# Second half of the output weights split during attention in the feed-forward's ring, and squares of head pairs added on GpSimd

## The chip, the cores and the metric

The kernel runs on one core of a Trainium2 chip, in one launch. A core has TensorE (PE) for matmuls, VectorE (DVE), ScalarE (ACT), GpSimd (POOL), and SyncE (SP), which here only issues transfers. The metric is the device time of the whole program in microseconds, the median of several executions.

## The reference

Two transformer blocks run one after the other on 512 tokens of width 1024, in float32. The change lies in the second:

```python
h = rmsnorm(x, norm_mix_w)
z = h @ w_in                       # u, v, q, keys, values, gates
a = gmlp_group(u, v, ...)          # 512 columns
b = nsa_group(q, k_c, v_c, k_s, v_s, k_w, v_w, g, ...)   # 8 heads of 64 = 512 columns
mix = concatenate([rmsnorm(a, out_norm_a_w), rmsnorm(b, out_norm_b_w)])
x = x + mix @ w_o                  # w_o is 1024 x 1024
h = rmsnorm(x, norm_ffn_w)
x = x + (silu(h @ w_gate) * (h @ w_up)) @ w_down
return rmsnorm(x, final_norm_w)
```

`nsa_group` adds three branches per head with gates: compressed keys, selected blocks, and a window. The rmsnorm of `b` needs the sum of the squares of all 512 columns of a token, so it is known only when the last head is done. The kernel multiplies by `out_norm_b_w` head by head and by the token's factor (`ssq`) after the product with `w_o`.

## The kernel before

**Split operands.** Every float32 matmul is done as three: an operand is split into a rounded part (hi) and the rest (lo), and hi*hi, lo*hi and hi*lo are added in PSUM (L174, L175, L176 in `mm3`). A weight tile arrives by a transfer into `raw` (issued on SP, L140), ACT casts it into `whi` (L116) and DVE, or GpSimd where `eng` says so, subtracts to get `wlo` (L117). `wload` does all of this for one tile of 512 KB. `set_wp` names the pools: a ring of raw tiles and a ring of hi/lo pairs; a transfer waits until its raw tile has been split, a cast until the matmuls that read its pair are done.

**Attention of the second block** (`block2`, `attn_run`). Eight heads, two branches each (`b`: selected, window), are 16 passes; each pass has four blocks of 128 queries, so there are 64 units. A unit is: scores `at` on PE, row maximum on DVE (L702, `amx`), exponential on ACT (L704, `pf`), reciprocal (L713, DVE), normalisation with the gate on GpSimd (L715), transposes `tr` on PE (L721), and the split of the transposed probabilities by ACT (L116, `PT`) and DVE (L117, `PT`). The values' matmuls into `po` follow once a pass. PE writes the scores of a unit up to three units ahead (three `at` banks). Work that is not attention is kept in the list `fill` and is put between units at the numbers that `B2A(left) = 4 + (11 - left) * 5` gives, `left` being the fillers left: queries of the last four heads (2), compressed keys of the second half (1), transposes of the gMLP part `mixA` (4) and its product with the first half of `w_o`, `out_a` (4). Eleven fillers stand at units 4, 9, ..., 54. A scheduler then orders each engine's instructions; the engine executes them in that order.

**After the attention.** `done` closes a head: squares `osq` (ACT), `oB` hi (ACT) and `oB` lo (DVE). Then a matmul with a column of ones sums `osq` over partitions and head pairs (L1843), DVE makes `ssq` (L1844, L240 to L249, L1846), and for each of four token tiles `out_half` makes two PSUM tiles of 12 matmuls (5 `acc` banks) with the second half of `w_o` (`wob`), DVE adds them to `x` (L1865), ACT squares and sums `x` (L1505, `rj`), DVE normalises (`hn`, L1508), PE transposes, ACT and DVE split into `h3T`. The feed-forward's first matmuls need `h3T` of three tiles. Its weights come through the ring `w5r` (3 raw tiles) and the pairs of `w5`; those of the first three feature blocks (6 tiles) are subtracted on GpSimd.

Of the kernel before, what the change touches and what calls it, by code (L numbers as in the profile page):

```python
# [17 lines left out]
OP = mybir.AluOpType  # L18
# [4 lines left out]
NT = S // P  # L23
# [30 lines left out]
class Net:  # L54
# [1526 lines left out]
    def block2(self, x3, out, pre):  # L1581

        nc, a, tc = self.nc, self.a, self.tc
# [5 lines left out]
        w1s, w1 = self.pool("w3", side="right")  # L1589
# [5 lines left out]
        for k0 in (0, 3, 6):  # L1595
            ks = slice(k0, min(k0 + 3, KD))
            n = ks.stop - k0
            raw = self.wraw([(src[:, ks, 1920:2048], slice(0, n), slice(0, P)),
                             (src[:, ks, 2176:2328], slice(0, n), slice(P, 280))], n, 280)
# [38 lines left out]
        for t in range(NT):  # L1638
            with tc.high_priority() if t == 0 else ExitStack():
                norm(t)  # L1640
                h = gp.tile([P, D], F, tag="hn", name=self.name("hn"), bufs=1)
# [87 lines left out]
        for t in range(NT):  # L1729
# [11 lines left out]
        half = lambda r: [[self.wload(wo[(4 * r + k0) * P:(4 * r + k0 + 2) * P, nb * 512:(nb + 1) * 512]  # L1741
                                      .rearrange("(c p) n -> p c n", p=P), 2, 512) for k0 in (0, 2)] for nb in range(2)]
        later = {}

        def queries(f):
            self.set_wp(wqp, 1024, 1, 2)
            self.proj_feat(hT, KD, w_in, [f], ev_q)
            if f == 11:
# [4 lines left out]
                self.set_wp(mx, 1024, 1, 4)  # L1753
                later["wo"] = half(0)

        def out_half(t, r, m, ch, evac):
            ts = slice(t * P, (t + 1) * P)
            for nb in range(2):
                ps = self.acc()
                for k in range(4):  # L1760
                    hi, lo = ch[nb][k // 2]
                    self.mm3(ps, (m[0][:, k, ts], m[1][:, k, ts]), (hi[:, k % 2], lo[:, k % 2]), k == 0, k == 3)
                evac(slice(nb * 512, (nb + 1) * 512), ps)

        def out_a(t):
            out_half(t, 0, later["mixA"], later["wo"],
                     lambda cs, ps: e.tensor_tensor(x3[:, t, cs], x3[:, t, cs], ps, op=OP.add))
# [4 lines left out]
        osq = ap.tile([P, 4, S], F, name="osq")  # L1772
        PT4 = [ap.tile([P, S], F, name=f"PT4{n}") for n in range(2)]

        def compressed(n):
# [24 lines left out]
            for qb in range(NT):  # L1800
# [3 lines left out]
        compressed(0)  # L1804
        each = lambda fn, it: [lambda i=i: fn(i) for i in it]
        fill = (each(queries, (10, 11)) + each(compressed, (1,)) + each(mixa, range(NT))
                + each(out_a, range(NT)))
        heads = []
        pos = {}
        for h in range(8):  # L1810
            n, g = h // 4, h % 4
            rows = slice((h % 2) * 64, (h % 2) * 64 + 64)
            pair = h // 2

            def po_(h=h):
                if h not in pos:
                    pos[h] = self.bank("po")[:64]
                return pos[h]

            def done(po, n=n, g=g, rows=rows, pair=pair):  # L1820
                nc.tensor.matmul(po, vcr[:, g, n], PT4[n], start=False, stop=True)
                nc.scalar.activation(osq[rows, pair], po, AF.Square)
                gcol = obT[rows, pair:pair + 1]
                nc.scalar.activation(oB[0][rows, pair], po, AF.Copy, scale=gcol)
                e.scalar_tensor_tensor(oB[1][rows, pair], po, gcol, oB[0][rows, pair].bitcast(F), op0=OP.mult,
                                       op1=OP.subtract)

            for b in range(2):
                def scores(ps, qs, m, stop, b=b, n=n, h=h):
                    nc.tensor.matmul(ps, QS[h][:, qs], KH[b][n][:, :m], start=True, stop=False)  # L1830
                    nc.tensor.matmul(ps, QS[h][:, qs], KL[b][n][:, :m], start=False, stop=stop)

                heads.append(dict(
                    scores=scores, po=po_, first=b == 0, last=False, done=done if b else lambda po: None,
                    v=lambda kb, b=b, n=n: tuple(VV[i][:, kb, b * P + n * 64:b * P + n * 64 + 64] for i in range(2)),
                    gate=lambda qb, b=b, h=h: gate[:, qb, 8 * (b + 1) + h:8 * (b + 1) + h + 1]))
# [2 lines left out]
        nc.gpsimd.memset(ones, 1.0)  # L1839
        pt = self.trp()  # L1840
        for t in range(NT):
            for c in range(4):
                nc.tensor.matmul(pt[:, t:t + 1], osq[:, c, t * P:(t + 1) * P], ones, start=c == 0, stop=c == 3)  # L1843
        e.tensor_scalar(ssq, pt[:, 0:NT], 1.0 / 512.0, 1e-6, op0=OP.mult, op1=OP.add)  # L1844
        rb = self.rsqrt(ssq, NT)
# [2 lines left out]
        g2s.close()  # L1848
        gms.close()
        cs_.close()  # L1850
        later["s"].close()
        self.set_ps(acc=5, tr=3)
        h3s, hp = self.pool("h3", side="right")
        hT = [hp.tile([P, KD, S], R, name=f"h3T{i}") for i in range(2)]

        w5rs, w5r = self.pool("w5r", side="right")
        w5 = [self.pool(f"w5{i}", side="right") for i in range(self.FP)]
        w1s, w1 = self.pool("w4")
        self.set_wp(w1, 1024, 3, 4)
        wob = half(1)  # L1860
        gs_, gp = self.pool("nrm2")
        gw = self.row(gp, A("norm_ffn_w")[0], D, "gffn")
        for t in range(NT):
            out_half(t, 1, oB, wob,
                     lambda cs, ps: e.scalar_tensor_tensor(x3[:, t, cs], ps, ssq[:, t:t + 1], x3[:, t, cs], op0=OP.mult,  # L1865
                                                           op1=OP.add))
            h = gp.tile([P, D], F, tag="hn", name=self.name("hn"), bufs=2)
            self.rms_tile(x3[:, t], D, gw, h, gp)
            self.to_T(h, hT[0], hT[1], t)
        gs_.close()  # L1870
        w1s.close()
        obs.close()
        w5 += [self.pool(f"w5{i}", side="right") for i in range(self.FP, 5)]
        self.set_wp([p for _, p in w5], 1024, self.FR, 10, rawpool=w5r)

        fs_, fp = self.pool("ff")
        fw = self.row(fp, a["final_norm_w_2"], D, "fnw")
# [28 lines left out]
            w = wd[f0 * P:(f0 + nf) * P]  # L1906
            self.proj_tok(hT2, nf, w, [0, 1], ev, ch=self.resident(nf, w, [0, 1]) if f0 else None)
        fs_.close()
        for st, _ in w5[::-1]:
            st.close()  # L1910
        w5rs.close()
        h3s.close()


@with_exitstack
# [32 lines left out]
```

## Time and profile before

| | |
|---|---|
| median of 3 runs | 2039.54 us (2037.53 to 2048.14) |
| the profiled execution | 2041.58 us |
| its span | 2039.9 us |
| mean granted TensorE clock | 0.950 |
| PE busy | 1851.5 us, 91% of the span |
| DVE busy | 1408.0 us, 69% |
| ACT busy | 1003.7 us, 49% |
| GpSimd busy | 557.8 us, 27% |

The span is the time from the first to the last instruction in the profile; the device time of that execution is 1.7 us longer. Times in rows are microseconds from the span's start. The second block's attention ends at about 1617 us, and its feed-forward runs from 1663 us to the end. PEclk 1.00 is TensorE's full 2.4 GHz, 0.50 is 1.2 GHz.

### The profile page before, as it was taken

Reading aid. Unit: us, or ns where it says so; the run is one execution under the profiler, and the core shown is the slowest. Engines: PE = TensorE matmul, PEld = TensorE weight load, DVE = VectorE, ACT = ScalarE, POOL = GpSimd, SP = SyncE. Lnnn points to the kernel's source line nnn. Section 1 sums busy time; section 2 is a strip of 40 time slices with the busy share of each in tenths; the row PEclk is TensorE's granted clock in tenths of the full one; section 3 lists DMA queues with packets and bytes.
Section 4 is the critical chain, followed back from the end, with each engine's and each line's share of the span. In section 5 each row is a group of like instructions: output and inputs, shape, how many; then the busy total and the mean of one; then the engine's idle time right before and its main releaser. Section 6 shows DMA issues by size and latency. Waiting matters only on the chain.

```text
span 2039.9 us, 25354 instructions
## 1 busy us (share of the span) xinstructions
PE 1851.5 (91%) x8971; PEld 1425.2 (70%) x8971; DVE 1408.0 (69%) x2610; ACT 1003.7 (49%) x1456; POOL 557.8 (27%) x459
## 2 busy tenths in 40 slices
PE   7699898998989998998989999759999799999998
PEld 6577676786766666666666666558777578888886
DVE  7966776777789888987888888574566563332333
ACT  3363555336337666765767766335355432222320
POOL 6633111200544433433443434230032300000000
PEclk8899999999989999998999999879989899999999
DMA  5223324633459999999999999724210243233311
GB/s 146 64 81 104 114 63 145 216 109 105 188 208 337 334 337 331 350 335 320 344 334 345 341 344 337 200 69 127 75 42 1 83 126 102 93 93 99 98 52 42
DMA packets 175580, 368.92 MB, mean 181 GB/s; under 512 B 17548, under 2 KB 113112, under 8 KB 150872
## 3 DMA queue, kind: packets, MB, share of 16 engines
q1 hardware_dynamic: 154240, 309.19, 44.5%
q0 software_dynamic: 17920, 52.98, 10.6%
q10 hardware_dynamic: 3288, 5.07, 0.8%
q8 instruction: 73, 1.20, 0.2%
q14 instruction: 59, 0.48, 0.1%
HBM read 337.83 MB, written 37.75 MB: 184 GB/s over the span
## 4 chain that ended last, share of the span: by engine, by line
PE 57%; DVE 16%; DMA 13%; ACT 7%; issue 5%; POOL 1%; another core or an unknown queue 1%; DVEq 0%; ACTq 0%; SPq 0%; POOLq 0%
PE acc L174 16%; PE acc L175 15%; PE acc L176 15%; DMA raw<-in_w_exp_gu_dram 5%; DVE wlo L117 3%; ACT whi L116 2%; DMA accd<-y,idx 2%; DMA gx<-x2d,idx 2%; PE tr L721 1%; PE tr L1263 1%; ACT xt L116 1%; DVE xt L117 1%; PE po L175 1%; PE po L176 1%; PE po L174 1%
## 5 line engine op out<-in xcount | busy, mean ns | idle before, releaser
L116 ACT CAST whi<-raw 128x1024 fp32r<-128x1024 f32 (+3 forms) x292 | 411.2, 1413 | 392.1 <-PE acc L175 196.1
L117 DVE TENSOR_TENSOR wlo<-raw,whi 128x1024 fp32r<-128x1024 f32 (+3 forms) x281 | 478.7, 1707 | 166.8 <-ACT whi L116 159.2
L1311 POOL DMA_INDIRECT accd<-y,idx x63 | 128.8, 2045 | 375.7 <-DMA accd<-y,idx 139.2
L174 PE MATMUL acc<-whi,gT 128*96 128x512 f32 x512 | 212.3, 415 | 0.0
L176 PE MATMUL acc<-whi,gT 128*96 128x512 f32 x512 | 207.6, 405 | 0.0
L175 PE MATMUL acc<-wlo,gT 128*96 128x512 f32 x512 | 206.8, 404 | 0.0
L1254 POOL DMA_INDIRECT gx<-x2d,idx x64 | 163.4, 2553 | 54.9 <-issue 16.7
L117 DVE TENSOR_TENSOR xt<-raw,xt 128x2048 fp32r<-128x2048 f32 x64 | 146.5, 2289 | 13.6 <-ACT xt L116 9.0
L174 PE MATMUL acc<-xt,aT 128*96 128x512 f32 x256 | 110.2, 430 | 42.0 <-ACT aT L116 41.8
L174 PE MATMUL acc<-h3T,whi 128*128 128x512 f32 (+2 forms) x368 | 140.5, 382 | 0.2 <-ACT h3T L116 0.2
L175 PE MATMUL acc<-h3T,whi 128*128 128x512 f32 (+2 forms) x368 | 140.5, 382 | 0.1
L176 PE MATMUL acc<-h3T,wlo 128*128 128x512 f32 (+2 forms) x368 | 140.5, 382 | 0.0
L116 ACT CAST xt<-raw 128x2048 fp32r<-128x2048 f32 x64 | 122.1, 1908 | 0.4
L176 PEld LDWEIGHTS acc<-whi,gT 128*96 128x96 f32 x512 | 85.5, 167 | 36.8 <-issue 1.1
L175 PEld LDWEIGHTS acc<-wlo,gT 128*96 128x96 f32 x512 | 86.2, 168 | 33.0 <-issue 0.2
L174 PEld LDWEIGHTS acc<-whi,gT 128*96 128x96 f32 x512 | 86.7, 169 | 32.3 <-issue 0.9
L1306 ACT ACTIVATE y<-acc,wsl 96x512 f32<-96x512 f32 x63 | 43.3, 687 | 126.2 <-PE acc L176 122.5
L175 PE MATMUL acc<-xt,aT 128*96 128x512 f32 x256 | 105.1, 411 | 0.0
L117 DVE TENSOR_TENSOR gT<-tr,gT 128x384 fp32r<-128x384 f32 x128 | 68.9, 549 | 40.6 <-ACT gT L116 40.4
L176 PE MATMUL acc<-xt,aT 128*96 128x512 f32 x256 | 90.7, 395 | 0.0
L174 PEld LDWEIGHTS acc<-xt,aT 128*96 128x96 f32 x256 | 42.8, 167 | 66.2 <-ACT aT L116 52.4
L116 ACT CAST gT<-tr 128x384 fp32r<-128x384 f32 x128 | 58.2, 480 | 55.5 <-PE tr L1263 55.5
(673 smaller groups left out, 4475.2 us busy)
## 6 DMA issues: line engine op xcount, KB each, us to landing
raw<-in_w_exp_gu_dram SPq DMA_DIRECT2D x128, 1024.0 KB, 9.6
raw<-in_w_exp_down_dram SPq DMA_DIRECT2D x64, 1024.0 KB, 10.6
raw<-in_w_in_dram SPq DMA_DIRECT2D x40, 512.0 KB, 4.1
raw<-in_w_gate_dram SPq DMA_DIRECT2D x22, 512.0 KB, 3.9
raw<-in_w_up_dram SPq DMA_DIRECT2D x22, 512.0 KB, 4.0
raw<-in_w_down_dram SPq DMA_DIRECT2D x22, 512.0 KB, 3.8
gsp<-sg POOLq DMA_DIRECT2D x16, 256.0 KB, 2.4
raw<-in_w_s_glu_dram SPq DMA_DIRECT2D x16, 256.0 KB, 4.2
```

What stands on the lines that cost most here:

```text
L116: first = nc.scalar.copy(hi, src)
L117: return first, (eng or nc.vector).tensor_tensor(lo, src, hi.bitcast(F), op=OP.subtract)
L174: mm(out, l[0], r[0], start=start, stop=False)
L175: mm(out, l[0], r[1], start=False, stop=False)
L176: mm(out, l[1], r[0], start=False, stop=stop)
L721: nc.tensor.transpose(pt[:, kb], pf[:, kb * P:(kb + 1) * P], self.ident)
L1254: nc.gpsimd.indirect_dma_start(out=gx, out_offset=None, in_=x2d, in_offset=bass.IndirectOffsetOnAxis(ap=idx, axis=0), bounds_check=S - 1, ...
L1263: nc.tensor.transpose(pt[:, c], gx[:, (c0 + c) * P:(c0 + c + 1) * P], self.ident[:C, :C])
L1306: nc.scalar.activation(y[:, :512], ps, AF.Copy, scale=w)
L1311: nc.gpsimd.indirect_dma_start(out=acc, out_offset=bass.IndirectOffsetOnAxis(ap=idx, axis=0), in_=y, in_offset=None, compute_op=OP.add)
```

## The change

`second` becomes a twelfth filler, the last one. It closes `mixA` (whose last reader is `out_a`), opens the feed-forward's raw ring and its first four hi/lo pairs in the freed space, and loads and splits the four tiles of the second half of `w_o` there; the feed-forward continues in the same ring with ten pairs. Since `B2A` counts fillers left, twelve fillers stand at units -1 (taken at the first), 4, ..., 54, so all eleven old ones move forward by five units and `second` takes unit 54. `squares`, called after head 5, adds `osq` of head pairs 0, 1 and 2 with two GpSimd additions of 128x512, so the ones-matmuls read 2 tiles instead of 4.

```diff
+        def second():
+
+            later["s"].close()
+            later["raw"] = self.pool("w5r", side="right")
+            later["w5"] = [self.pool(f"w5{i}", side="right") for i in range(self.FP)]
+            self.set_wp([p for _, p in later["w5"]], 1024, self.FR, 4, rawpool=later["raw"][1])
+            later["wob"] = half(1)
+
+        def squares():
+            nc.gpsimd.tensor_tensor(osq[:, 0], osq[:, 0], osq[:, 1], op=OP.add)
+            nc.gpsimd.tensor_tensor(osq[:, 0], osq[:, 0], osq[:, 2], op=OP.add)
...
-                + each(out_a, range(NT)))
+                + each(out_a, range(NT)) + [second])
...
+                if h == 5:
+                    squares()
...
-            for c in range(4):
+            for c in (0, 3):
...
-        later["s"].close()
...
-        w5rs, w5r = self.pool("w5r", side="right")
-        w5 = [self.pool(f"w5{i}", side="right") for i in range(self.FP)]
-        w1s, w1 = self.pool("w4")
-        self.set_wp(w1, 1024, 3, 4)
-        wob = half(1)
+        w5rs, w5r = later["raw"]
+        w5 = later["w5"] + [self.pool(f"w5{i}", side="right") for i in range(self.FP, 5)]
+        self.set_wp([p for _, p in w5], 1024, self.FR, 10, rawpool=w5r)
+        self.wslot = 2 * self.FP - 1
+        wob = later["wob"]
```

**ACT near the end of the attention.** These are rows of the changed kernel: `at_15304` and `at_15321` are the last two units of head 6's first pass, `at_15355` to `at_15437` its second pass, `at_15466` on head 7; `raw_15413`, `15419`, `15425`, `15431` are the four tiles of `w_o`.

```order
L704 ACTIVATE pf_15327,amx_15325<-at_15321,amx_15325 128x512
L116 CAST whi_15415<-raw_15413 128x1024
L704 ACTIVATE pf_15361,amx_15359<-at_15355,amx_15359 128x128
L116 CAST whi_15421<-raw_15419 128x1024
L1834 ACTIVATE osq<-po_15232 64x512
L1836 ACTIVATE oB_12871<-po_15232,obT 64x512
L116 CAST PT_15329<-tr_15365 128x256
L704 ACTIVATE pf_15376,amx_15374<-at_15370,amx_15374 128x256
L116 CAST PT_15329<-tr_15380 128x384
L116 CAST whi_15427<-raw_15425 128x1024
L116 CAST PT_15329<-tr_15396 128x512
L704 ACTIVATE pf_15392,amx_15390<-at_15386,amx_15390 128x384
```

No `whi` stood there before; the four casts of this half of `w_o` stood behind the last `oB` of the attention. The fourth (`whi_15433`) comes right after these rows, ahead of the exponential of `at_15437`.

**DVE at the same place, changed kernel.** These are the subtractions of the same four tiles among the units' maxima (L702) and splits (`PT`).

```order
L117 TENSOR_TENSOR wlo_15416<-raw_15413,whi_15415 128x1024
L713 RECIPROCAL amx_15359<-amx_15359 128x1
L117 TENSOR_TENSOR wlo_15422<-raw_15419,whi_15421 128x1024
L1837 SCALAR_TENSOR_TENSOR oB_12872<-po_15232,obT,oB_12871 64x512
L117 TENSOR_TENSOR PT_15330<-tr_15365,PT_15329 128x256
L117 TENSOR_TENSOR PT_15330<-tr_15380,PT_15329 128x384
L702 TENSOR_REDUCE amx_15390<-at_15386 128x1
L117 TENSOR_TENSOR wlo_15428<-raw_15425,whi_15427 128x1024
L117 TENSOR_TENSOR PT_15330<-tr_15396,PT_15329 128x512
L117 TENSOR_TENSOR wlo_15434<-raw_15431,whi_15433 128x1024
L702 TENSOR_REDUCE amx_15441<-at_15437 128x1
```

Before, these four subtractions stood behind `ssq` (L1846), three ahead of the first addition to `x` (L1865) and one ahead of the second.

**DVE between the second and the third token tile's `hn`, changed kernel.** `wlo_16219`, `16250`, `16286` and `16317` are weights of the feed-forward (tiles 7 to 10 of its order); `hn_15806` is tile 1.

```order
L1508 SCALAR_TENSOR_TENSOR hn_15806<-x_12783,rs_15811,gffn 128x1024
L1878 SCALAR_TENSOR_TENSOR x_12784<-acc_15852,ssq,x_12784 128x512
L117 TENSOR_TENSOR wlo_16219<-raw_16216,whi_16218 128x1024
L117 TENSOR_TENSOR h3T_15703<-tr_15824,h3T_15702 128x4x128
L117 TENSOR_TENSOR h3T_15703<-tr_15831,h3T_15702 128x4x128
...
L117 TENSOR_TENSOR wlo_16250<-raw_16247,whi_16249 128x1024
...
L117 TENSOR_TENSOR wlo_16286<-raw_16283,whi_16285 128x1024
...
L117 TENSOR_TENSOR wlo_16317<-raw_16314,whi_16316 128x1024
```

Tile 2's `hn` stands ten rows behind the last of these. Before, no weight stood between the `hn` of tile 1 and that of tile 2; two of the feed-forward's stood ahead of the `hn` of tile 0.

## Rows read from the trace of the kernel before

**Rows 1.** Windows: length, PE, PEld, DVE, ACT, POOL busy (instructions), clock, DMA.

```profile
1591.50:1596.60 5.10, 5.10 (x38) 3.81 (x37) 3.58 (x9) 2.86 (x10) 0.77 (x1) 1.00 0.78 210
1596.60:1617.40 20.80, 16.84 (x80) 10.78 (x79) 7.99 (x24) 8.57 (x24) 4.83 (x8) 0.84 0.31 101
...
1620.00:1625.00 5.00, 2.20 (x8) 1.60 (x8) 3.49 (x4) 3.89 (x5) 3.45 (x2) 0.50 0.00 1
1625.00:1630.00 5.00, 0.00 (x0) 0.00 (x0) 4.83 (x6) 1.05 (x1) 4.48 (x3) 0.50 0.36 104
1630.00:1635.00 5.00, 1.25 (x3) 1.05 (x4) 4.79 (x10) 0.00 (x0) 1.36 (x1) 0.50 0.13 6
1635.00:1640.00 5.00, 5.00 (x13) 3.86 (x13) 2.12 (x3) 1.26 (x2) 0.00 (x0) 0.52 0.99 283
1645.00:1650.00 5.00, 5.00 (x23) 4.03 (x22) 4.67 (x13) 3.32 (x6) 0.75 (x1) 1.00 0.82 233
```

**Rows 2.** PE in time order: start, duration, operation, count, idle before and its releaser.

```profile
1591.23 0.40 PE L176 MATMUL acc<-whi,mixA 128*128 128x512 f32 x1
1591.47 0.39 PE L1830 MATMUL at<-KH,QS 128*128 128x512 f32 x1
1596.61 0.31 PE L1830 MATMUL at<-KH,QS 128*128 128x128 f32 x1
1604.13 0.76 PE L721 MATMUL tr<-ident,pf 128*128 128x128 f32 x5 [1.20 <-DVE PT L117]
1605.43 0.48 PE L174 MATMUL po<-PT,VV 128*64 128x512 f32 x1 [0.54 <-ACT PT L116]
1606.16 0.69 PE L175 MATMUL po<-PT,VV 128*64 128x512 f32 x1 [0.25 <-DVE PT L117]
1617.43 3.98 PE L1843 MATMUL tr<-ones,osq 128*128 128x1 f32 x26 [0.68 <-ACT osq L1822]
1633.76 0.79 PE L175 MATMUL acc<-wlo,oB 128*128 128x512 f32 x1 [10.91 <-DVE wlo L117]
1663.22 0.62 PE L174 MATMUL acc<-h3T,whi 128*128 128x384 f32 x2 [0.24 <-ACT h3T L116]
1668.15 1.06 PE L292 MATMUL tr<-ident,hn 128*128 128x128 f32 x8
```

**Rows 3.** DVE in time order, from the squares' sum to the third tile's norm.

```profile
1621.64 2.28 DVE L240 TENSOR_SCALAR rs<-ssq 128x4 f32<-128x4 f32 x1
1632.40 0.17 DVE L1846 COPY ssq<-rs 128x4 f32<-128x4 f32 x1
1632.48 3.50 DVE L117 TENSOR_TENSOR wlo<-raw,whi 128x1024 fp32r<-128x1024 f32 x3
1660.49 1.28 DVE L1508 SCALAR_TENSOR_TENSOR hn<-x,rs,gffn 128x1024 f32<-128x1024 f32 x1
```

**Rows 4.** POOL in time order: the feed-forward's first six weights.

```profile
1621.55 6.95 POOL L117 TENSOR_TENSOR wlo<-raw,whi 128x1024 fp32r<-128x1024 f32 x3 [14.18 <-ACT whi L116]
1640.98 4.77 POOL L117 TENSOR_TENSOR wlo<-raw,whi 128x1024 fp32r<-128x1024 f32 x2 [9.62 <-ACT whi L116]
```

**Rows 5.** Groups by shape (busy us, mean ns): tail's ACT, then DVE and ACT after it.

```profile
L116 ACT CAST PT<-tr 128x512 fp32r<-128x512 f32 x4 | 2.3, 586 | 2.1 <-PE tr L721 2.1
L704 ACT ACTIVATE pf<-at,amx 128x512 f32<-128x512 f32 x3 | 2.1, 694 | 0.6 <-DVE amx L702 0.4 <-DVE amx L713 0.2
...
L117 DVE TENSOR_TENSOR wlo<-raw,whi 128x1024 fp32r<-128x1024 f32 x7 | 8.4, 1221 | 0.3 <-ACT whi L116 0.2
L1865 DVE SCALAR_TENSOR_TENSOR x<-acc,ssq,x 128x512 f32<-128x512 f32 x8 | 6.0, 747 | 6.5 <-PE acc L176 6.4
L117 DVE TENSOR_TENSOR h3T<-tr,h3T 128x512 fp32r<-128x512 f32 x8 | 5.2, 687 | 2.3 <-ACT h3T L116 2.2
L116 ACT CAST whi<-raw 128x1024 fp32r<-128x1024 f32 x7 | 7.3, 1052 | 12.1 <-DMA raw<-in_w_o_dram 9.0 <-DMA raw<-in_w_up_dram 2.3 <-DMA raw<-in_w_gate_dram 0.8
```

**Rows 6.** The page's DMA issues: count, KB each, median us from issue to landing.

```profile
raw<-in_w_gate_dram SPq DMA_DIRECT2D x22, 512.0 KB, 3.9
```

More of the change, by code (lines that the diff above doesn't have):

```diff
@@ L1818, in po_, with done @@
                 return pos[h]
-            def done(po, n=n, g=g, rows=rows, pair=pair):
+            def done(po, n=n, g=g, rows=rows, pair=pair, h=h):
                 nc.tensor.matmul(po, vcr[:, g, n], PT4[n], start=False, stop=True)
@@ L1870, in block2 @@
         gs_.close()
-        w1s.close()
         obs.close()
-        w5 += [self.pool(f"w5{i}", side="right") for i in range(self.FP, 5)]
-        self.set_wp([p for _, p in w5], 1024, self.FR, 10, rawpool=w5r)
         fs_, fp = self.pool("ff")
@@ L1908, in block2 @@
         fs_.close()
-        for st, _ in w5[::-1]:
+        for st in [st for st, _ in w5[:self.FP - 1:-1]] + [h3s] + [st for st, _ in w5[self.FP - 1::-1]] + [w5rs]:
             st.close()
-        w5rs.close()
-        h3s.close()
 @with_exitstack
```

## The prediction

> **What bounds the kernel now.** The page first: PE is busy for 91% of the span, so what can be won is where PE waits or runs at the low clock. The windows show one such place, the seam between the second block's attention and its feed-forward [rows 1]: from 1620 to 1635 PE works 3.45 of 15 us, from 1635 to 1640 it is full but at a clock of 0.52 (13 matmuls where 1645 to 1650 has 23). Before it, in the attention's tail, PE works 16.84 of 20.8 us at 0.84; once the feed-forward runs, nothing is left to win. PE in time order says what ends each wait [rows 2]: the tail's gaps end on DVE and ACT splits of probabilities (1.20, 0.54, 0.25), the last ones-matmuls start at 1617.43 and their 26 records take 3.98 us, and the product with the second half of w_o waits 10.91 us for the first `wlo`. That wait is the one the change aims at. DVE in time order shows what stands before that `wlo` [rows 3]: a chain of operations on 128x4 numbers for `ssq`, one of them 2.28 us, ready at 1632.57, and only then three `wlo`. GpSimd runs the feed-forward's `wlo` meanwhile [rows 4]. So the wait has two causes in series, `ssq` and the splits; taking the splits away leaves `ssq`, and everything that leads to the feed-forward's first matmul (additions to x, norms, transposes) needs `ssq` too.
>
> **The change, part by part.** I count on the axis of the profiled execution: 2041.58 us, of which the span is 2039.9; it lies 2.0 us above the median, to which the sum is carried over at the end. All casts of a weight are 1.05 us on ACT and all its subtractions 1.22 us on DVE [rows 5].
>
> **1. The seam after the attention.** Let the last ones-matmuls start at the same 1617.43. The 26 records become 14 (half of the 16 matmuls), 2.1 us at the same 0.153 each: 1.8 us earlier. PE then goes straight into the product: its weights are there. But DVE's `ssq` chain stands beside GpSimd's first `wlo` as before: these began at 1621.55, right behind the ones-matmuls [rows 4], and the chain was done 11.0 us later. Now they begin at about 1619.2, behind the first cast, and run as before; so `ssq` at 1630.2 instead of 1632.57.
> From there to tile 2's `hn` I add DVE's queue as its order stands: six additions 0.75, two finished tiles' `h3T` 4 x 0.69, three `hn` 1.28, four weights of the feed-forward 1.22 (they now stand there, before they didn't), the last tile's two additions, some 35 small operations at 0.17: 4.5 + 2.8 + 3.8 + 4.9 + 1.5 + 6.0 = 23.5, and two waits of about 1.2 for ACT's `rj`, since tile 1's second addition now stands behind tile 0's `hn`. That is 1656 to 1657, against 1661.8 [rows 3]. PE has 60 product matmuls done by the first `hn` (five banks) and waits for DVE from there; DVE has the pace, and the four splits taken away were replaced by four others. The first feed-forward matmul follows 1.45 us behind, as before (1663.22): 1658.3. Tile 3's `hn` is next in DVE's queue, so its transposes are done by 1659.8, where before their 1.0 us stood inside the feed-forward, at 1668.15. So the feed-forward flows from 1659.8 instead of 1664.2: **-4.4**.
> Two things take from that. PE waits some 7 us for tile 2 (1649.5 to 1656.8). After the wait of 10.91 the clock was at 0.50 and the next 5 us had 13 matmuls instead of 23 [rows 1]; at the feed-forward's start the same costs 2.2 to 2.9 us: **+2.5** (0 to 2.9). And GpSimd's fifth and sixth `wlo`, 4.77 us, which ran beside DVE's second product waits before [rows 4], now fall on tile 0's norm, because ACT casts them only behind the first `rj`: **+1** (0 to 4.8).
> The 128x4 operations that took 2.28 beside GpSimd's `wlo` and 0.17 without it [rows 3, 4] agree with the Trainium skill, "SBUF — State Buffer", section "SBUF: two separate sides": DVE and GpSimd share a port pair as an exclusive lock, and the loser is blocked for the whole instruction. By that rule alone the last term would be the full +4.8; the additions from PSUM at 1640 to 1645 of 0.75 show no such delay.
>
> **2. The tail of the attention.** The transfers of w_o go into the space of `mixA`, whose last reader is the end of `out_a`; there is no reading them earlier. With the fillers five units forward, `out_a` ends 43 PE instructions earlier, about 4.5 us of matmuls (rows of 512 columns stand 0.24 apart, the rest in proportion): at 1587.0 instead of 1591.5. Call this T. A tile of 512 KB takes 3.9 us to land [rows 6]: T+4.3. ACT reaches the first cast at T+3.4 and waits 0.9. From there its queue has, in order, cast, exponential, cast, squares, copy, two splits with an exponential between, cast, split, exponential, cast: with 0.6 to 0.9 for an exponential and 0.3 to 0.6 for a split [rows 5], the exponential of the unit before head 7 ends at T+9.4 and the fourth cast at T+13.4. DVE's fourth `wlo` ends at T+14.6, the maximum queued behind it at 15.3, its exponential at 16.2. PE's scores run three units ahead and each needs the exponential of three units before: it waits for the first of these 2.9 us, for splits 0.9 and 0.7, for the last exponential 1.7. I get PE to head 7's second pass at T+17.9. Before, that score stood at 1596.61 [rows 2]; the same PE work from T is 4.5 + 5.1 = 9.6 with no wait (PE 5.10 of 5.10 [rows 1]). Loss 8.3; but the tail after it had waits of 1.20 + 0.54 + 0.25 on the same engines, which a PE that comes later doesn't meet again: **+6.3**. Lower bound: in those 5.1 us ACT was free for 2.2 and DVE for 1.5 [rows 1], the passes around have as much, and if the units in flight absorb the rest, +1. Upper bound: no wait is saved and the landing is late, +10.
> The low clock began in the tail at about 1605, after these gaps [rows 1, 2]; with larger gaps earlier, it begins earlier, beside waits that hide part of it: **+1** (0 to 8).
>
> **3. The rest.** `squares` are two GpSimd operations of half a weight's size, 2.32 / 2 = 1.2 us each by [rows 4], one of them in the stretch just counted, where GpSimd is nearly idle (0.77 of 5.1): 0, at most +1 through what it holds up. The fillers' forward move at the attention's start, where PE is full, and the second compressed part, whose DVE chain has less PE work before its transposes: **+0.5** (0 to 2.5). The feed-forward's ring with six pairs ahead: nothing, PE is full there before.
>
> Sum: -4.4 + 2.5 + 1 + 6.3 + 1 + 0.5 = +6.9; since I may count waits twice where ACT and DVE are late together, I take **+6**: 2047.6 for the profiled execution, **2045.5** by the median.
>
> **The rivals.** *PE has the pace at the seam (faster).* If DVE's weights and small operations slip between PE's, the seam is 96 product matmuls at 0.234 (22.5 us), 2.8 for those at the low clock, four tiles of transposes (4.2), 2.1 and 1.5 at the ends: 1617.43 + 33.1 = 1650.5 against 1664.2, -13.7, with the tail at its lower bound +1 and 0.5 for the rest: 2027.3. For it: the wait of 10.91 is the largest of this stretch. Against: DVE was busy 4.67 of 5 us from 1645 [rows 1] and gets no less work. It decides from -12 at the seam. Chance 0.13.
> *The low clock spreads through the tail (slower).* If the first wait of 2.9 us at T+6.5 brings the clock down and the tail never gets it back, the matmuls of the tail that ran at full speed before (some 7.5 us up to 1605, and 3.7 of the stretch before) take twice as long where no wait hides it: up to +11 in place of +1, which with waits beside it I put at +8: 2052.5. From 4.5 us of such loss on it is slower by over 0.5%. For it: 1605 to 1617 ran low although PE was busy most of the time. Chance 0.22.
> *The splits vanish in the tail, and the seam is DVE's (no change).* Tail +1, seam -1 to -4: 2036 to 2040. It is part of the forecast's case: together 0.65.
>
> **How the numbers follow.** 0.5% is 10.2 us, about what a measurement of this kernel can tell from no change. Faster by more 0.13, within 0.65, slower by more 0.22. The terms' lower bounds (seam -4.4 or a little below with the lock not met, tail +1) give 2036, their upper bounds 2058; the faster rival lies at 2027. 8 in 10 lie between 2030 and 2055.
>
> **What the profile of the changed kernel would show.** The wait of 10.91 is gone and the product starts behind the ones-matmuls; if it stays, part 1 is wrong from its start. DVE is busy without a break from `ssq` to tile 2's `hn`, and PE waits there for `hn`; if PE is full, the first rival is right. In the tail, the four `whi` end between T+5 and T+14 and PE waits 5 to 9 us more than before between `out_a` and the last ones-matmuls, which start near 1624; if they start by 1619, part 2 is wrong. The clock at the feed-forward's first 5 us: half by my count. A tail at 0.5 from some 1594 on is the second rival.

## The result and the profile after

The change is slower. In six runs of each the changed kernel took 2059.12 us (median, 2051.81 to 2060.5), the kernel before 2040.24 (2037.53 to 2048.14); the ratio on record is 1.0066, 95% interval 1.0045 to 1.0087, that is +13.5 us (+9 to +18). The profiled execution took 2055.44 us, 13.9 more than that of before. The two medians lie 18.9 us apart, 0.93%, just outside that interval, so the size is less certain than the direction; what follows goes by the ratio and the profiles. The forecast was +6, within 0.5%; slower by more than 0.5%, where the ratio lies, had a chance of 0.22.

For every kernel of this study the second block can be cut at four instructions: the first mask matmul of the compressed keys, the last matmul of `out_a`, the last group of ones-matmuls, and the first feed-forward matmul. The lengths between them, each the difference of two starts in PE's time order, in us:

| kernel | to out_a's end | out_a's end to ones | attention, sum | ones to feed-forward | feed-forward to end |
|---|---|---|---|---|---|
| before | 124.8 | 26.2 | 151.0 | 45.8 | 376.7 |
| changed | 124.8 | 38.2 | 163.0 | 45.8 | 377.5 |

The attention is 12.0 us longer, the seam (ones to feed-forward) no shorter, the feed-forward 0.9 longer; the other 0.9 of the 13.9 lies ahead of the second block's attention, where nothing was changed.

The attention can be cut further, at the mask matmul of the second half's compressed keys and at the first score of head 7's second pass. PE in these four stretches, before (length, busy, instructions, clock, DMA share and GB/s):

```profile
1466.39:1499.66 33.27, 33.25 (x183) 0.90 0.16 48
1499.66:1591.23 91.57, 87.60 (x504) 0.94 0.06 18
1591.23:1596.61 5.38, 5.38 (x39) 1.00 0.74 200
1596.61:1617.43 20.82, 16.83 (x81) 0.84 0.31 100
```

And in the changed kernel:

```profile
1467.28:1495.20 27.92, 26.44 (x139) 0.88 0.21 57
1495.20:1592.12 96.92, 91.72 (x507) 0.91 0.05 17
1592.12:1608.95 16.83, 13.33 (x79) 1.00 0.70 218
1608.95:1630.32 21.37, 17.09 (x80) 0.84 0.01 2
```

About as many instructions stand between the second compressed keys and `out_a`'s end in both (504 and 507), and they take 5.3 us longer: PE is busy for 4.1 us more, at a lower mean clock, and idle for 1.2 more. The instructions that the forward move took away ahead of the keys make that stretch 5.4 us shorter; where they stand now, between `out_a`'s end and head 7's second pass, they make it 11.5 us longer. The rest of the tail is 0.6 us longer.

PE of the changed kernel in time order, with idle time ahead and its releaser:

```profile
1507.96 1.12 PE L1813 MATMUL tr<-ident,p 128*128 128x128 f32 x4 [2.38 <-DVE p L1809]
...
1592.12 0.40 PE L176 MATMUL acc<-whi,mixA 128*128 128x512 f32 x1
...
1601.12 0.33 PE L1844 MATMUL at<-KH,QS 128*128 128x128 f32 x1 [1.31 <-ACT pf L704]
1602.92 0.44 PE L174 MATMUL po<-PT,VV 128*64 128x512 f32 x1 [0.45 <-ACT PT L116]
...
1607.17 0.44 PE L1844 MATMUL at<-KH,QS 128*128 128x384 f32 x1 [1.14 <-ACT pf L704]
...
1617.04 0.77 PE L721 MATMUL tr<-ident,pf 128*128 128x128 f32 x5 [1.20 <-DVE PT L117]
...
1630.32 1.72 PE L1857 MATMUL tr<-ones,osq 128*128 128x1 f32 x14 [0.68 <-ACT osq L1834]
...
1653.91 1.97 PE L292 MATMUL tr<-ident,hn 128*128 128x128 f32 x8 [7.85 <-DVE hn L1508]
...
1674.40 1.94 PE L292 MATMUL tr<-ident,hn 128*128 128x128 f32 x8 [5.87 <-DVE rs L249]
1676.16 0.69 PE L174 MATMUL acc<-h3T,whi 128*128 128x384 f32 x1
1676.69 1.94 PE L292 MATMUL tr<-ident,hn 128*128 128x128 f32 x8
```

The wait of 10.91 us for the first `wlo` [rows 2] is gone, and the product starts behind the ones-matmuls. In its place PE waits 7.85 us for tile 0's norm and 5.87 for tile 2's (the row names `rs`, which DVE worked on next; tile 2's `hn` ends at 1674.26). DVE of the changed kernel in time order shows what those norms waited for:

```profile
1632.28 2.31 DVE L240 TENSOR_SCALAR rs<-ssq 128x4 f32<-128x4 f32 x1
...
1636.97 2.32 DVE L247 TENSOR_TENSOR rs<-rs 128x4 f32<-128x4 f32 x1
...
1639.72 2.34 DVE L247 TENSOR_TENSOR rs<-rs 128x4 f32<-128x4 f32 x1
...
1643.09 0.17 DVE L1860 COPY ssq<-rs 128x4 f32<-128x4 f32 x1
...
1647.16 2.18 DVE L245 SCALAR_TENSOR_TENSOR rs<-rs,rs 128x1 f32<-128x1 f32 x1
1649.37 2.26 DVE L249 SCALAR_TENSOR_TENSOR rs<-rs,rs 128x1 f32<-128x1 f32 x1
1651.67 0.22 DVE L245 SCALAR_TENSOR_TENSOR rs<-rs,rs 128x1 f32<-128x1 f32 x1
...
1664.58 1.23 DVE L117 TENSOR_TENSOR wlo<-raw,whi 128x1024 fp32r<-128x1024 f32 x1 [1.73 <-ACT whi L116]
...
1670.95 1.22 DVE L117 TENSOR_TENSOR wlo<-raw,whi 128x1024 fp32r<-128x1024 f32 x1
...
1672.98 1.28 DVE L1508 SCALAR_TENSOR_TENSOR hn<-x,rs,gffn 128x1024 f32<-128x1024 f32 x1
```

GpSimd's instructions beside them, in the same view of the same kernel:

```profile
1632.18 7.09 POOL L117 TENSOR_TENSOR wlo<-raw,whi 128x1024 fp32r<-128x1024 f32 x3 [11.90 <-PE tr L1857]
1639.64 2.40 POOL L117 TENSOR_TENSOR wlo<-raw,whi 128x1024 fp32r<-128x1024 f32 x1 [0.37 <-ACT whi L116]
1646.98 4.64 POOL L117 TENSOR_TENSOR wlo<-raw,whi 128x1024 fp32r<-128x1024 f32 x2 [4.93 <-DVE rs L241]
```

`ssq` is ready 12.9 us after the ones-matmuls began (before: 15.1 [rows 2, 3]). GpSimd's fifth and sixth subtraction now stand right on the chain of tile 0's norm: the same operation takes 2.18 us beside them and 0.22 behind them. Last, windows of 5 us of the changed kernel at the attention's start, with the sum over 1465 to 1530, and at the feed-forward's (columns as in [rows 1]):

```profile
1495.00:1500.00 5.00, 4.42 (x38) 4.30 (x37) 2.92 (x11) 2.33 (x9) 2.93 (x5) 0.91 0.30 105
1500.00:1505.00 5.00, 4.46 (x16) 3.26 (x17) 3.38 (x5) 1.65 (x4) 0.00 (x0) 0.50 0.00 0
1505.00:1510.00 5.00, 2.62 (x12) 2.05 (x11) 3.90 (x10) 1.93 (x4) 0.70 (x1) 0.50 0.30 105
1510.00:1515.00 5.00, 4.68 (x15) 2.98 (x15) 1.44 (x5) 2.72 (x7) 1.20 (x2) 0.50 0.34 105
...
sum 65.00, PE 58.71 PEld 43.98 DVE 37.97 ACT 32.62 POOL 11.88; mean PE 4.52 PEld 3.38 DVE 2.92 ACT 2.51 POOL 0.91
...
1675.00:1680.00 5.00, 5.00 (x21) 4.57 (x20) 4.06 (x7) 2.35 (x4) 0.00 (x0) 0.50 0.31 83
```

And the kernel before at the attention's start, in the same windows:

```profile
1500.00:1505.00 5.00, 5.00 (x39) 4.70 (x37) 2.74 (x9) 3.15 (x8) 2.00 (x4) 0.83 0.38 105
1505.00:1510.00 5.00, 5.00 (x21) 3.89 (x21) 3.85 (x8) 1.41 (x3) 0.00 (x0) 0.50 0.34 101
1510.00:1515.00 5.00, 2.57 (x13) 1.68 (x13) 4.30 (x11) 2.74 (x7) 1.73 (x2) 0.84 0.06 7
...
sum 65.00, PE 61.90 PEld 48.36 DVE 42.10 ACT 37.58 POOL 18.89; mean PE 4.76 PEld 3.72 DVE 3.24 ACT 2.89 POOL 1.45
```

The compressed keys of the second half, 32 columns to a matmul, stand at 1495 to 1501 in the changed kernel and at 1500 to 1504 in that before. Behind them the clock is at 0.50 for three windows in the one, for one window in the other, and PE is idle 6.3 of the 65 us instead of 3.1. The feed-forward of the changed kernel, too, begins at 0.50, behind PE's wait for tile 2.

### The profile page after: what moved, and what is told of

It is laid out like the page before. It is cut to its first block, busy times and chain, and to the rows that moved or that the text cites. A ratio compares the mean times of both kernels' runs of the same rounds, so it can differ in the third digit from the quotient of the medians.

```text
span 2053.7 us, 25334 instructions
## 1 busy us (share of the span) xinstructions
PE 1858.2 (90%) x8955; PEld 1426.8 (69%) x8955; DVE 1412.1 (69%) x2610; ACT 1003.4 (49%) x1456; POOL 560.0 (27%) x461
## 4 chain that ended last, share of the span: by engine, by line
PE 59%; DVE 15%; DMA 11%; ACT 8%; issue 5%; POOL 2%; another core or an unknown queue 1%; ACTq 0%; DVEq 0%; SPq 0%; POOLq 0%
PE acc L174 17%; PE acc L175 16%; PE acc L176 16%; DMA raw<-in_w_exp_gu_dram 6%; ACT whi L116 3%; DVE wlo L117 2%; DMA gx<-x2d,idx 2%; PE tr L1263 1%; PE tr L721 1%; DVE xt L117 1%; ACT xt L116 1%; DMA accd<-y,idx 1%; PE po L175 1%; PE tr L292 1%; DVE rs L245 1%
## 5 line engine op out<-in xcount | busy, mean ns | idle before, releaser
L117 DVE TENSOR_TENSOR gT<-tr,gT 128x384 fp32r<-128x384 f32 x128 | 68.8, 548 | 36.7 <-ACT gT L116 36.7
```

The costliest lines, as they stand in the source:

```text
L117: return first, (eng or nc.vector).tensor_tensor(lo, src, hi.bitcast(F), op=OP.subtract)
```

## The experiments

The theory that the trace after suggests: three places lose, each by its own cause. The forward move of the fillers costs at the attention's start, the splits of w_o cost in the tail, and at the seam GpSimd's subtractions and four weights of the feed-forward eat what the earlier splits gain. Rivals: one of the two, forward move or splits, is the whole loss; or the short DVE operations are long for another reason.

One profile does not tell small differences in the attention from chance. Three kernels without early splits and with the fillers in their old units have 151.0 us (before), 149.4 (`e4_squares`) and 150.1 (`e8_sq_dve`); three with early splits and the old units have 150.5 (`e2_keep`), 152.7 (`e7_keep_dve`) and 152.4 (`e11_six`).

**Fillers forward alone** (`e1_shift`), on the kernel before:

```diff
-                + each(out_a, range(NT)))
+                + each(out_a, range(NT)) + [lambda: None])
```

> The kernel before with a twelfth filler that does nothing, so that the eleven others stand five units earlier as in the change; the loads and splits of w_o and the squares stay where they were. Theory (three places: start of the attention +5, tail +8 by the splits of w_o, seam +1): the start's loss alone shows, out_a ends about 5 us later than its five units' move would give, the tail is 5 units longer without fillers and loses 0 to 2 more, so 2045 to 2048, 0.25% to 0.4% over before. Rival (the tail's loss comes from its having no filler for ten units, not from the splits): all of the start's and tail's loss is here, 2052 to 2054. Rival (the forward move costs nothing, the splits do all): 2040.

Measured 1.0039 (1.0024 to 1.0054), +8 us; the attention is 156.8 us, +5.8. So the forward move alone costs about half of the 12.0 us lost in the attention, with no split of w_o in it: the second rival is out, and the first, which expected all of the loss here, is not met either. PE in the four stretches of this kernel:

```profile
1466.81:1493.49 26.68, 25.03 (x139) 0.94 0.21 60
1493.49:1588.96 95.47, 89.72 (x506) 0.93 0.06 18
1588.96:1603.97 15.01, 13.25 (x82) 1.00 0.69 210
1603.97:1623.62 19.65, 15.53 (x81) 0.91 0.00 1
```

The stretch behind the compressed keys is 3.9 us longer than before. The displaced instructions add 9.6 us to the tail (15.01 instead of 5.38) and take 6.6 off the stretch ahead of the keys.

**Splits without the move** (`e2_keep`), on the changed kernel:

```diff
-                + each(out_a, range(NT)) + [second])
+                + each(out_a, range(NT - 1)) + [lambda: (out_a(NT - 1), second())])
```

> The changed kernel with the eleven old fillers at their old units and the loads and splits of w_o called in unit 54, right behind the last out_a. Theory: the start's 5 us are back, the tail still has ACT's and DVE's splits and waits for its transfers: 2045 to 2049, 0.25% to 0.45% over before. Rival (forward move is the whole loss): 2038 to 2041. Rival (the splits are the whole loss): 2052 to 2054 as the changed kernel.

Measured 1.0009 (0.9997 to 1.0021). The attention is 150.5 us, not longer than before: out_a's end to the ones-matmuls grew by 1.3, and the stretch before it was shorter by 1.8. The expected 2045 to 2049 was too much. By the six attentions named above the splits alone cost 1.7 us on average, about what single profiles differ by; the rival, that the forward move is the whole loss, is nearer for the attention. The seam is 45.9, as in the changed kernel.

**Squares alone** (`e4_squares`), the two GpSimd additions and the shorter ones-matmuls on the kernel before:

> The kernel before with the squares alone. Theory: the ones-matmuls take 2 us less, GpSimd's first weight and the ssq chain begin 2 us earlier, the wait for the first wlo ends earlier by the same: 2037 to 2039. Rival (the chain is set by GpSimd's casts, not by the ones-matmuls, or the two additions hold up the attention): 2040 to 2042.

Measured 0.9982 (0.9971 to 0.9993), -3.7 us. The profile has 2.9 us of it at the seam (42.9 instead of 45.8): `ssq` follows 12.7 us behind the start of the ones-matmuls instead of 15.1.

**No subtraction on GpSimd** (`e6_dve`), on the changed kernel:

```diff
-                    hi, lo = self.wload(..., KD, P, eng=nc.gpsimd if f0 + fi < 3 else None)
+                    hi, lo = self.wload(..., KD, P, eng=None)
```

> The changed kernel with the feed-forward's first six subtractions on DVE and none on GpSimd. Theory (DVE's short operations wait out GpSimd's subtractions): ssq is ready 5 us after the ones-matmuls begin instead of 12.9, the first tile's norm loses its two operations of 2.2 us, but DVE gets six times 1.22: tile 2's norm ends some 38 us after the ones-matmuls instead of 43.9, so 5 to 6 us less than the changed kernel. Rival (the long operations are slow for another reason, such as a wait inside DVE): ssq stays at 12 to 13 and the six subtractions come on top, 5 to 7 us more than the changed kernel.

Measured 1.0009 (0.9995 to 1.0023): 11.7 us less than the change by the two ratios (1.0066 - 1.0009 = 0.0057 of 2044), more than the 5 to 6 expected. The profiles explain 9.3: ones to feed-forward 37.3 instead of 45.8, and 376.8 instead of 377.5 behind it. DVE in time order:

```profile
1633.97 0.17 DVE L1860 COPY ssq<-rs 128x4 f32<-128x4 f32 x1
...
1647.80 1.28 DVE L1508 SCALAR_TENSOR_TENSOR hn<-x,rs,gffn 128x1024 f32<-128x1024 f32 x1
1653.09 1.28 DVE L1508 SCALAR_TENSOR_TENSOR hn<-x,rs,gffn 128x1024 f32<-128x1024 f32 x1
1663.12 1.28 DVE L1508 SCALAR_TENSOR_TENSOR hn<-x,rs,gffn 128x1024 f32<-128x1024 f32 x1
```

The ones-matmuls began at 1629.00, so `ssq` took 5.1 us instead of 12.9. With six more subtractions of 1.22 us in its own queue, DVE still has tile 2's norm 8.5 us earlier behind the ones-matmuls (34.1 instead of 42.7). The rival (slow for another reason) is out. The remaining 2.4 us of the 11.7 are within the two intervals.

**Both repairs** (`e7_keep_dve`): the old fillers' units and no subtraction on GpSimd, on the changed kernel.

> The changed kernel with the old fillers at their old units (as the second run) and the feed-forward's first six subtractions on DVE (as the fourth). Theory: the two repairs are in different places and add up, the attention ends as in the second run, some 2 us behind the kernel before, and the seam is 8 to 9 us shorter than the change's: 9 to 11 us less than before, ratio 0.9945 to 0.9955. Rival (DVE, which now has all subtractions, takes back at the seam what the old fillers give): 0.998 to 1.001.

Measured 0.9972 (0.9956 to 0.9989), -5.7 us, between the two expectations. Ones to feed-forward is 39.3, and tile 2's norm comes 10.4 us after tile 1's: four weights of the feed-forward stand between them.

**The same on the kernel before with squares** (`e8_sq_dve`): w_o stays behind the attention.

> The kernel before with the squares and with the feed-forward's first six subtractions on DVE; the loads of w_o stay behind the attention. Theory: ssq is ready 5 us after the ones-matmuls begin instead of 12.6, but in DVE's order three of the six stand ahead of the first wlo of w_o, and three behind it: of the 7.6 us some 4 are given back before the product starts and 3 behind, so 0 to 2 us less than the squares alone, ratio 0.997 to 0.9985. Rival (without GpSimd's subtractions the seam shortens by the whole 7.6 here too): 0.994.

Measured 0.9962 (0.9943 to 0.9982), -7.8 us, more than the theory gave; ones to feed-forward 38.7, 4.2 less than with the squares alone. So with GpSimd out of the way, and four weights of the feed-forward still between the norms in `e7_keep_dve`, the early splits of w_o bring nothing at the seam that late ones don't (38.7 here, 39.3 there).

**The first three fillers forward** (`e9_start`) and **the last eight forward** (`e10_tail`), on the kernel before:

```diff
-    B2A = staticmethod(lambda left: 4 + (11 - left) * 5)
+    B2A = staticmethod(lambda left: 4 + (11 - left) * 5 - 5 * (left > 8))     # e9_start
+    B2A = staticmethod(lambda left: 4 + (11 - left) * 5 - 5 * (left <= 8))    # e10_tail
```

> The kernel before with only the first three fillers (the last queries and the second half's compressed keys) five units earlier; the other eight stay. Theory: the start's part of the forward move, two waits and a longer stretch at the low clock around the compressed keys, 2 to 5 us: ratio 1.001 to 1.0025; the tail is as before. Rival (the forward move costs only because the tail has no filler): 1.000.

> The kernel before with only the last eight fillers (the transposes and out_a) five units earlier; the first three stay. Theory: the tail is 5 units longer without fillers, from out_a's end to the ones-matmuls 34 to 35 us instead of 26.2 plus the 4.5 that moved there, so 3 to 4.5 us: ratio 1.0015 to 1.0025. Rival (the start alone): 1.000.

Measured 1.0025 (1.0003 to 1.0047) and 0.9992 (0.9977 to 1.0008). In the profiles the first comes to `out_a`'s end 4.6 us later than before and gets 2.9 back in the tail: +1.7 for the attention. The second comes there 9.0 us earlier and has a tail of 36.3 us: +1.1. The two parts sum to 2.8, the whole move costs 5.8, and with the splits 8.8 to 12.0 (163.0, 162.8 and 159.8 us in the changed kernel, `e6_dve` and `e12_six_after`). In the profiles the parts don't add up to the whole; by the times, +5.1 us (+1 to +10) and -1.6 (-5 to +2) against +8 (+5 to +11), they may. By the timed runs the start is the part that costs; the expected loss of the tail alone was not found.

**Weights 7 to 10 behind the norms** (`e12_six_after` on the changed kernel; `e11_six` the same on `e7_keep_dve`): the feed-forward's first half uses six pairs of the ring and leaves w_o's four alone.

```diff
                 for w in (wg, wu):
+                    if not f0 and self.wslot == 2 * len(w5) - 1:
+                        self.wslot = 2 * self.FP - 1
```

> The changed kernel with that one edit: weights 7 to 10 of the feed-forward are split behind the norms; fillers, squares and GpSimd's subtractions as in the change. Theory: tile 2's norm starts 35 to 37 us after the ones-matmuls instead of 42.7; 6 to 8 us less than the changed kernel, ratio 1.0025 to 1.004. Rival (GpSimd's six subtractions alone set the seam): 1.006 as the change.

> The kernel of the seventh run (old fillers in place, no subtraction on GpSimd) whose feed-forward leaves the four pairs of w_o alone until its second half, so that its weights 7 to 10 are split only when the first pairs come free, behind all four norms. Theory (four subtractions of 1.22 us and the waits for their casts stand between tile 1's and tile 2's norm and delay the feed-forward): tile 2's norm starts some 6 us earlier, 30 instead of 36 us after the ones-matmuls; 5 to 7 us less than the seventh run, ratio 0.993 to 0.995. Rival (DVE only gets the same work later and the feed-forward waits for its weights instead): 0.997 to 1.000.

Measured 1.0026 (1.0011 to 1.0041), as expected, and 0.9955 (0.9931 to 0.9978), -9.2 us, just outside the expected 0.993 to 0.995. Ones to feed-forward is 40.8 instead of 45.8, and 31.8 instead of 39.3. By the times the edit is worth 8.2 us on the changed kernel and 3.5 on `e7_keep_dve`, whose interval overlaps with that of `e11_six`. By the profiles the seam gains 5.1 and 7.5; on the changed kernel 3.2 more lie in the attention, which the edit does not touch. In `e11_six` PE has no wait above 1.41 us there:

```profile
1622.36 1.72 PE L1857 MATMUL tr<-ones,osq 128*128 128x1 f32 x14 [0.68 <-ACT osq L1834]
...
1642.53 1.09 PE L292 MATMUL tr<-ident,hn 128*128 128x128 f32 x8 [1.41 <-DVE rss L1506]
...
1652.88 1.06 PE L292 MATMUL tr<-ident,hn 128*128 128x128 f32 x8 [1.37 <-DVE hn L1508]
1654.18 0.62 PE L174 MATMUL acc<-h3T,whi 128*128 128x384 f32 x2 [0.24 <-ACT h3T L116]
```

The rival (the feed-forward waits for its weights instead) is out: its length to the end is 376.7 and 376.6. The clock of `e11_six` is 1.00 from 1630 on.

Is it the early splits that pay here? `e8_sq_dve`, which has none, measured 0.9962 against 0.9955, and the intervals overlap: the times don't show that they do. In the profiles `e11_six` is 6.9 us shorter at the seam and 2.3 longer in the attention.

**w_o's subtractions in the tail on GpSimd** (`e13_six_pool`, on `e11_six`):

> The first kernel of this group with the four subtractions of w_o's second half, in the attention's tail, on GpSimd instead of DVE. GpSimd is idle there for most of the time. Theory (DVE and GpSimd block one another, and the normalisations of the units queue behind 2.34 us each): the tail, out_a's end to the ones-matmuls, gets 2 to 6 us longer than the 28 of the seventh run, ratio 0.995 to 0.998. Rival (DVE's queue was what delayed the tail): 1 to 2 us shorter, 0.992 to 0.994.

Measured 0.9953 (0.9934 to 0.9972): the same as `e11_six`. The profile has the tail 2.4 us longer (30.6 instead of 28.2), with PE waiting 3.15 us for a normalisation that queued behind two subtractions:

```profile
1603.87 0.47 PE L721 MATMUL tr<-ident,pf 128*128 128x128 f32 x1 [3.15 <-POOL pf L715]
```

That agrees with the theory in the one profile; the times can't tell the two apart.

## Why the prediction was right in direction and short in size

By the ratio on the prediction's 2039.54 the changed kernel takes 2053.0 us, inside the range of 2030 to 2055; its own median of 2059.12 lies above. That the ratio falls inside is partly luck: the upper end was made of the tail and its clock (+10 and +8), while most of what was missing came from a term put at +0.5. The terms' upper bounds, added up as they stand, give +23.8 or 2063, not 2058.

**The seam: the wait for `wlo` went, as said, and DVE kept the pace.** `ssq` at 12.8 us behind the ones-matmuls was foreseen (1630.2 - 1617.4); measured 12.9 to its copy's end. Foreseen for tile 2's norm was an end 39.4 us behind, measured 43.9 (1674.2 - 1630.3). Most of the difference of 4.5 is the term "GpSimd's fifth and sixth `wlo` ... now fall on tile 0's norm: +1 (0 to 4.8)". It was mis-sized: 2.18 + 2.26 us for two operations that take 0.22 and 0.16 alone is 4.1. DVE also waited 1.73 us for a cast ahead of the first of the four weights, which the sum had not; its small operations took less than the 6.0 counted. The Trainium skill, "SBUF — State Buffer", "SBUF: two separate sides", would have had the full term, since by its rule a DVE operation with two SBUF inputs and an instruction of GpSimd block one another, each for the whole length of the one that starts first; the trace agrees with it: two DVE operations of one number per partition, both with two SBUF operands, each waited out a GpSimd subtraction of 2.3 us. I had set it low because additions beside GpSimd's subtractions were not delayed before; those read PSUM, and were no evidence for operations that read SBUF twice. `e6_dve` then showed what GpSimd's six subtractions cost the seam: with their work on DVE it is 8.5 us shorter. The first rival, PE with the pace, was wrong for the change; `e11_six` shows what it takes to come near it (31.8 us against its 33.1).

**The low clock at the feed-forward's start** came as said, 21 instructions at 0.50 from 1675 to 1680, but the feed-forward to the end is 0.9 us longer where the sum had +2.5. The 1.0 us that the sum gained by having tile 3's transposes done ahead of the feed-forward did not come: they stand behind its first matmul, at 1676.69.

**The tail: right in size, only half right in cause.** Foreseen from `out_a`'s end to the ones-matmuls were 36.7 us (17.9 + 20.8, less the 2.0 of waits not met again), 37.7 with the clock's +1; measured 38.2 (16.8 + 21.4). But the sum put +6.3 on ACT's and DVE's splits of w_o and took the displaced matmuls at 4.5 us. In `e1_shift`, without any split, these take 9.6 us in the tail, which is 34.7 us long. The splits add 3.5 us to that in the changed kernel, and 1.3 to 2.2 where the fillers stand in their old units (`e2_keep`, `e7_keep_dve`, `e11_six`). PE's idle time between `out_a` and the ones-matmuls grew by 3.8 us (7.8 instead of 4.0), not by 5 to 9. The ones-matmuls started at 1630.3 and not near 1624, since `out_a` had not ended earlier.

**The attention's start: the step that failed.** "The fillers' forward move at the attention's start ... +0.5 (0 to 2.5)". With the move `out_a` should have ended 4.5 us earlier and ended at the same 124.8. The stretch between the second compressed keys and `out_a`'s end, with as many instructions as before, is 5.3 us longer, and 3.9 in `e1_shift`; in `e9_start`, which moves the first three fillers alone, `out_a` ends 4.6 us later. Of the 5.3 us, 4.1 are PE busy for longer, at a mean clock of 0.91 instead of 0.94, and 1.2 are idle time. The windows of 5 us show where: behind the second half's compressed keys three windows stand at 0.50 instead of one. I counted DVE's chain there (PE's wait behind it is 2.38 us) and not the clock. Why the clock stays low for longer when the keys come five units earlier, no run shows.

**The squares** stood in the sum as an `ssq` that is ready 2.4 us earlier (1630.2 instead of 1632.57); alone they gave 2.4 there (12.7 instead of 15.1) and 2.9 at the seam by the profile.

Of the rivals, the slower one came nearest in size (its 2052.5), but not by its mechanism: the tail's clock was 1.00 up to head 7's second pass and 0.84 behind it, as before, and the low clock that mattered was at the start. What stays open is why the start's and the tail's part of the forward move cost 2.8 us apart and 5.8 together in the profiles, and how exactly the 12.0 us divide: the move alone has 5.8, the splits alone 1.7, and the three profiles with both have 8.8 to 12.0, so that 1.3 to 4.5 come only with both or are chance.

## What to carry to other kernels

A table that counts fillers from the end moves all of them when one is appended; check what leaves the stretch that they covered before pricing what enters it. When a wait for an operand is removed, look at what else stands on the queue that produced it: here DVE set the pace at the seam of the changed kernel, and with the early splits in place the seam got shorter only when other work was taken off DVE's chain (GpSimd's subtractions beside it, the next stage's weights in it). Compare the repaired kernel with one that has the repair and not the change: `e11_six` gained 9.2 us, but `e8_sq_dve` gained 7.8 without any early split. Short operations on DVE are dear beside long ones on GpSimd that make them wait: 0.2 us became 2.3.

## What the runs showed of the hardware

In the changed kernel five DVE operations on 128x1 and 128x4 numbers took 2.18 to 2.34 us each, each beside a GpSimd subtraction of 128x1024; operations of the same kind took 0.16 to 0.22 without one. Moving six such subtractions of 2.3 to 2.4 us from GpSimd to DVE, 1.22 us each there, took 8.5 us off the seam and made the kernel 11.7 us faster by the ratios. TensorE's granted clock was 0.50 from 1500 to 1515 of the changed kernel; ahead of that, in a window with a group of 32-column matmuls, PE was busy for 4.42 of 5 us.
